# Second layer's input projection as a seven-product scheme, and its output projection as one sum

## The chip, the cores and the metric

One core of one Trainium2 chip. The metric is the device time of one execution in microseconds (us), median of the runs shown. TensorE (PE) multiplies, VectorE (DVE), ScalarE (ACT) and GpSimd (POOL) do everything else on chip, and SyncE's queue (SP) issues most transfers.

## The reference, cut to what matters

Layer 1 (counted from 0) is the retention layer, and the change is there: h is 1024 tokens x 1024 features, w_in 1024 x 6144, w_out 2048 x 1024, with 4 heads whose q and k are 256 and v and g 512 wide. Layer 0 (differential attention) is not touched, but its last steps build the input of layer 1.

```python
def retention(h, w_in, w_out):
    proj = jnp.einsum("bsd,de->bse", h, w_in)
    q, k, v, g = jnp.split(proj, [1024, 2048, 4096], axis=-1)
    ...
    inner_out = jnp.einsum("bnhij,bnjhe->bnihe", inner, v)
    _, cross = lax.scan(step, state0, ...)
    out = head_rms_norm(inner_out + cross)
    y = jax.nn.silu(g.astype(f32)) * out
    return jnp.einsum("bse,ed->bsd", y.astype(h.dtype), w_out)

for layer in range(DEPTH):
    h = rms_norm(x, pre_gain[layer]) * (1.0 + scale) + shift
    y = mixer(h)
    x = x + gate * rms_norm(y, post_gain[layer])
```

## The kernel before, in words

Every float32 product is made of three fp16 products: each operand is split into a high part (`hi`, written by ACT) and a low part (`lo`, what is left, written by DVE), and the pairs hi-hi, hi-lo and lo-hi are added up in PSUM. A product over 1024 rows of the contraction is therefore 8 blocks x 3 = 24 matmuls of 128x128 weights and 512 moving columns.

Layer 0 ends with its output projection: `out0(t)` for 8 tiles of 128 tokens, 48 matmuls each (`outproj`, L551), then `residual`, a store of the new rows to DRAM (`x1_d`, a DMA issued by POOL) and their norm. `out0_hT(g)` (g = 0, 1: tiles 0 to 3 and 4 to 7) transposes the rows on PE (L297), and `modulate` applies scale and shift (ACT) and splits (ACT, DVE) into the tiles `hT`. The order of these steps is a string of letters (`order`); inside it, and everywhere else, a list scheduler fixes one order of instructions per engine when the kernel is built. Each engine then runs its own list first in, first out, and waits at a row whose inputs or buffers aren't ready.

Layer 1 works head by head (`retain`), two heads a half:
- `qk_T`: queries and keys of the head, 8 products of 24 matmuls with the weights stationary (`proj_T`, L306), N = 512 tokens;
- for each of six spans of tokens (`SPANS`): `scores` (L744), `values` (the v projection of a tile, `proj_N`, L318, 24 matmuls), `state` (L764) and `outputs` (L785, L795);
- `gate`: the g projection of each of 8 tiles (L318 again), then SiLU, times the output, and the split.

Layer 1's input projection is thus 4 heads x (8 + 8 + 8) x 24 = 2304 matmuls of 512 columns. Line 318 has 2304 in all as well, by chance: 1536 of them are layer 1's, and 768 of L306's 1392.

After each half, `out1_yT` transposes y by DMA and `outproj` multiplies with that half's 1024 rows of `ret_w_out`; half 0 writes its sum to DRAM (`part_d`), half 1 loads it, adds it (L865) and finishes with `residual`. That is 2 x 8 x 48 = 768 matmuls of 512 columns.

Buffers matter below: PSUM has banks `mm` (3), `sc` (2), `tr` (1), `av` (2), one 128x512 float32 each. In SBUF a `tag` is a ring of `bufs` slots, and a tile waits until its slot's last reader is done: the attention tiles `v` and the residual rows `xres` share the tag `v` (2 slots).

Of the kernel before, what the change touches and what calls it, by code (L numbers as in the profile page):

```python
# [79 lines left out]
def trunk(ctx: ExitStack, tc: tile.TileContext, a: dict, out: bass.AP):  # L81
# [4 lines left out]
    raws = ctx.enter_context(tc.tile_pool(name="raws", bufs=2))  # L86
    ws = ctx.enter_context(tc.tile_pool(name="ws", bufs=2))
    hts = ctx.enter_context(tc.tile_pool(name="hts", bufs=1))
    ys = ctx.enter_context(tc.tile_pool(name="ys", bufs=1))
    rows = ctx.enter_context(tc.tile_pool(name="rows", bufs=2))  # L90
    dram = ctx.enter_context(tc.tile_pool(name="dram", bufs=1, space=DRAM))
# [25 lines left out]
    part_d = dram.tile([P, NT, D], F32, name="part_d")  # L117
# [101 lines left out]
    def ada_gate(l, j):  # L219
# [108 lines left out]
    l0 = ctx.enter_context(ExitStack())  # L328
    att = l0.enter_context(tc.tile_pool(name="att", bufs=2, reuse_waits="tile"))
# [568 lines left out]
```

## Time and profile before

| | |
|---|---|
| median of 3 runs | 1398.25 us (1396.84 to 1399.16) |
| the profiled execution | 1397.34 us, span 1395.6 us |
| PE busy | 1337.2 us (96%) |
| DVE, ACT, POOL busy | 797.1 us (57%), 593.3 us (43%), 140.5 us (10%) |
| mean granted clock of PE | 0.995 |

The span is from the first to the last instruction; the 1.7 us beside it lie around the program. The share of busy time says which engine has no room; what ended an engine's idle time is read from the waits, and what a step takes from the timeline of its stretch.

### The profile page before, as it was taken

The numbers are of one execution on the slowest core, as the hardware profiler recorded it, in microseconds if no ns is written. First come the engines' busy times: TensorE is split into PE (matmuls) and PEld (weight loads), VectorE is DVE, ScalarE is ACT, GpSimd is POOL, SyncE is SP. The second block draws the span as 40 slices with busy tenths as digits, with TensorE's granted clock in tenths as the row PEclk, the third lists the DMA queues.
The fourth block names the chain that finished last, engine by engine and source line by source line (L and its number), as shares of the span: only waits on it lengthen the run. The fifth ranks groups of instructions, "written<-read, shape, count | busy, mean of one in ns | idle before, by whom it ended". The sixth has DMA issues, their size and how long they took to land.

```text
span 1395.6 us, 18378 instructions
## 1 busy us (share of the span) xinstructions
PE 1337.2 (96%) x7049; PEld 652.5 (47%) x7049; DVE 797.1 (57%) x1636; ACT 593.3 (43%) x1160; POOL 140.5 (10%) x278
## 2 busy tenths in 40 slices
PE   3899999999999998999999999999999999999997
PEld 2445455445545444444444444444444444444443
DVE  4866996997887777563663255420126632554443
ACT  4854544653644655473452234321224422343211
POOL 2000110101101222210000000100000000000011
PEclk9999999999999999999999999999999999999999
DMA  9823554556442466642310230334333102304274
GB/s 301 246 66 70 131 119 113 146 128 135 102 129 52 120 153 131 169 146 89 98 54 15 76 99 0 94 94 120 99 99 99 47 18 76 98 1 121 61 196 136
DMA packets 230953, 148.23 MB, mean 106 GB/s; under 512 B 141721, under 2 KB 219729, under 8 KB 230865
## 3 DMA queue, kind: packets, MB, share of 16 engines
q1 hardware_dynamic: 226608, 131.84, 35.9%
q0 software_dynamic: 4256, 15.21, 3.3%
q8 instruction: 55, 0.90, 0.3%
q14 instruction: 34, 0.27, 0.1%
HBM read 99.85 MB, written 12.58 MB: 81 GB/s over the span
## 4 chain that ended last, share of the span: by engine, by line
PE 79%; DVE 9%; ACT 3%; DMA 3%; issue 3%; SPq 2%; POOL 1%; DVEq 0%; POOLq 0%; ACTq 0%
PE ps_mm L318 32%; PE ps_mm L306 16%; PE ps_mm L551 16%; DMA dT<-sb 2%; PE ps_mm L795 2%; PE ps_sc L764 2%; PE ps_av L785 2%; PE ps_av L523 2%; DVE sb L493 2%; PE ps_sc L489 2%; PE ps_sc L490 1%; DVE acc L160 1%; DVE sb L512 1%; PE ps_sc L744 1%; DVE sb L508 1%
## 5 line engine op out<-in xcount | busy, mean ns | idle before, releaser
L318 PE MATMUL ps_mm<-w,hT 128*128 128x512 f16 x2304 | 513.1, 379 | 0.0
L318 PEld LDWEIGHTS <-hT 128*128 128x128 f16 x2304 | 223.6, 98 | 257.6
L306 PE MATMUL ps_mm<-hT,w 128*128 128x512 f16 x1392 | 309.9, 379 | 0.8 <-ACT po L856 0.8
L551 PE MATMUL ps_mm<-w_o,yT 128*128 128x512 f16 x1152 | 256.2, 380 | 0.1
L306 PEld LDWEIGHTS <-w 128*128 128x128 f16 x1392 | 135.4, 98 | 157.4 <-ACT w L246 0.8
L551 PEld LDWEIGHTS <-yT 128*128 128x128 f16 x1152 | 112.6, 98 | 133.1 <-issue 2.8
L247 DVE SCALAR_TENSOR_TENSOR w<-raw,w 128x2048 f16<-128x2048 f32 (+1 forms) x52 | 92.1, 1794 | 92.1 <-ACT w L246 92.1
L500 ACT ACTIVATE sb<-sb,mx 128x128 f32<-128x128 f32 (+7 forms) x128 | 98.2, 768 | 64.0 <-DVE mx L493 63.5
L493 DVE CUSTOM_DVE_ANT_0 sb<-ps_sc,table 128x512 f32<-128x512 f32 (+3 forms) x128 | 73.3, 585 | 34.2 <-PE ps_sc L490 29.1
L246 ACT ACTIVATE w<-raw 128x2048 f16<-128x2048 f32 (+1 forms) x52 | 76.9, 1511 | 27.9 <-PE ps_mm L318 10.1
L489 PE MATMUL ps_sc<-ks,qs 128*128 128x512 f16 (+3 forms) x192 | 61.5, 327 | 5.8 <-DVE mx L493 5.6
L511 ACT ACTIVATE sb<-sb 128x896 f16<-128x896 f32 (+6 forms) x64 | 43.3, 679 | 55.8 <-DVE sb L508 55.6
L160 DVE SCALAR_TENSOR_TENSOR acc<-raw,cond,acc 128x256 f32<-128x256 f32 x140 | 65.7, 480 | 2.1
L523 PEld LDWEIGHTS <-dT 128*128 128x128 f16 x864 | 53.6, 99 | 27.3 <-DMA dT<-sb 18.7
L279 POOL TENSOR_SCALAR ss<-ss 128x1 f32<-128x1 f32 x48 | 15.6, 324 | 473.4 <-ACT junk L278 462.4
L490 PE MATMUL ps_sc<-kl,qs 128*128 128x512 f16 (+3 forms) x192 | 61.7, 327 | 0.0
L830 DVE TENSOR_TENSOR sg<-y,sg 128x512 f32<-128x512 f32 x32 | 22.1, 690 | 69.0 <-ACT sg L813 69.0
L725 ACT ACTIVATE vr<-ps_mm 128x512 f16<-128x512 f32 x32 | 19.1, 597 | 91.6 <-PE ps_mm L318 91.6
L726 DVE SCALAR_TENSOR_TENSOR vr<-ps_mm,vr 128x512 f16<-128x512 f32 x32 | 22.1, 689 | 62.9 <-ACT vr L725 62.9
L523 PE MATMUL ps_av<-v,dT 128*128 128x128 f16 x756 | 52.7, 219 | 5.4 <-DMA dT<-sb 5.4
L813 ACT ACTIVATE sg<-ps_mm 128x512 f32<-128x512 f32 x32 | 19.1, 597 | 90.1 <-PE ps_mm L318 90.1
L512 DVE SCALAR_TENSOR_TENSOR sb<-sb 128x896 f16<-128x896 f32 (+6 forms) x64 | 48.2, 754 | 10.9 <-ACT sb L511 10.8
(165 smaller groups left out, 1412.3 us busy)
## 6 DMA issues: line engine op xcount, KB each, us to landing
raw<-in_ret_w_in SPq DMA_DIRECT2D x24, 1024.0 KB, 5.4
raw<-in_ada_w SPq DMA_DIRECT2D x32, 512.0 KB, 6.8
raw<-in_da_w_in SPq DMA_DIRECT2D x16, 1024.0 KB, 5.5
raw<-in_ada_w SPq DMA_DIRECT2D x8, 1024.0 KB, 5.2
raw_o<-in_ret_w_out SPq DMA_DIRECT2D x8, 1024.0 KB, 5.0
x<-in_x SPq DMA_DIRECT2D x8, 512.0 KB, 7.5
raw_o<-in_da_w_out SPq DMA_DIRECT2D x4, 1024.0 KB, 5.2
xres<-in_x POOLq DMA_DIRECT2D x4, 1024.0 KB, 7.2
```

The costliest lines, as they stand in the source:

```text
L160: nc.vector.scalar_tensor_tensor(out=acc, in0=t[:, k, :], scalar=cond[:, k : k + 1], in1=acc, op0=ALU.mult, op1=ALU.add)
L246: nc.scalar.activation(out=hi, in_=t[:, k, :], func=AF.Copy, scale=SW)
L247: nc.vector.scalar_tensor_tensor(out=lo, in0=t[:, k, :], scalar=SW, in1=hi, op0=ALU.mult, op1=ALU.subtract)
L306: nc.tensor.matmul(ps, w[:, k, wi, lo : lo + P], hT[k][g][:, xi, :], start=(k == 0 and wi == 0 and xi == 0), stop=(k == NK - 1 and wi == 1),)
L318: nc.tensor.matmul(ps, hT[k][g][:, xi, j * P : (j + 1) * P], w[:, k, wi, :], start=(k == 0 and wi == 0 and xi == 0), stop=(k == NK - 1 and ...
L489: nc.tensor.matmul(ps[c][:, 0:n], qs[:, c, q], ks[:, c, k], start=True, stop=False)
L490: nc.tensor.matmul(ps[c][:, 0:n], qs[:, c, q], kl[c][:, k], start=False, stop=True)
L493: nc.vector.tensor_tensor_reduce(out=sb[:, c, k], in0=ps[c][:, 0:n], in1=table[:, S - L + lo : S - L + lo + n], scale=-es, scalar=(3.0e38 ...
L500: nc.scalar.activation(out=sb[:, c, 0:L], in_=sb[:, c, 0:L], func=AF.Exp, scale=-1.0, bias=mx[:, m0 + c : m0 + c + 1], accum_out=z[:, 4 * ...
L512: nc.vector.scalar_tensor_tensor(out=dh[:, 1, :], in0=sb[:, 0, 0:L], scalar=SD, in1=dh[:, 0, :], op0=ALU.mult, op1=ALU.subtract)
L523: nc.tensor.matmul(o[:, i * P : (i + 1) * P], dT[:, di * (t + 1) + kb, :], v[:, kb, vi, e], start=(kb == 0 and di == 0 and vi == 0), stop= ...
L551: nc.tensor.matmul(ps, yT(yi, k), wo[k // 4][:, k % 4, wi, n * 512 : (n + 1) * 512], start=(k == 0 and yi == 0 and wi == 0), stop=(k == NK ...
```

## The change

Layer 1's input projection is made of seven products of quarters where the plain scheme has eight. The 1024x1024 matrix h is cut in four quarters (512 features x 512 tokens: `A11`, `A12`, `A22` and the sums `N3`, `S1`, `M2`, `N4`; even tiles of 128 tokens are one half, odd tiles the other). A block of weights, 1024 rows x 512 columns (`Columns`: q and k of a head, or the two halves of its v, or of its g), is cut in four quarters of 512x256, with the sums `T1` to `T4`. `Quarters.product(n)` does one of the seven products; some share a PSUM bank (`chain` x, y, z) and go on adding where the last stopped, after ACT has copied the bank out (`kept`). Four results are put together by DVE additions.

- Per product and per half of its outputs: 4 blocks x 3 = 12 matmuls of 512 columns for q and k of heads 1 to 3; for head 0 (tokens in two groups) and for all v and g, 24 matmuls of 256 columns.
- The sums of weights are made by POOL, in float32, in the loaded blocks: four 128x1024 additions per `Columns` (`prepare`), 12 `Columns` in all. Blocks are split by ACT and DVE (128x1024 each, 7 per `Columns`); B22 is loaded twice. Weights are made ready three products ahead (`AHEAD`), loads start up to six ahead.
- The sums of h are made by DVE in `out0_hT`, in tiles `hq` that take the tag `v`, in place of `modulate`.
- v and g of a head are computed for all 8 tiles; the retention steps then run beside g's products, one span after each product.
- The output projection is one sum over 2048 rows at the end. `y` of heads 0 to 2 goes to DRAM (`y_d`) and comes back by DMA transposes from there; the last head's y is transposed from SBUF. `part_d`, its store, its loads and L865 are gone. `ret_w_out` comes in 16 loads of 512 KB, 8 MB in all, just ahead of it.

```diff
+        for k in range(4):
...
+            t = att.tile([P, 8, 256], F32, name="hq", tag="v", bufs=2)
...
+                nc.scalar.activation(out=t[:, 2 * i : 2 * i + 2], in_=ps, func=AF.Identity, scale=m[:, 1:2], bias=m[:, 0:1])
+            nc.vector.tensor_tensor(
+                out=t[:, 4:6], in0=t[:, 1:2].to_broadcast([P, 2, 256]), in1=t[:, 0:4:3], op=ALU.subtract
+            )
+            nc.vector.tensor_tensor(out=t[:, 6], in0=t[:, 0], in1=t[:, 5], op=ALU.subtract)
+            nc.vector.tensor_tensor(out=t[:, 7], in0=t[:, 2], in1=t[:, 6], op=ALU.subtract)
+            for src, dst, sign in (
+                (t[:, 0:4:3], lambda b: hA[k // 2][:, k % 2, :, b, n], -1.0),
+                (t[:, 2], lambda b: hB[0][:, k, b, n], 1.0),
+                (t[:, 4:8], lambda b: hS[k][:, :, b, n], 1.0),
+            ):
+                nc.scalar.activation(out=dst(0), in_=src, func=AF.Copy, scale=sign)
+                nc.vector.scalar_tensor_tensor(out=dst(1), in0=src, scalar=sign, in1=dst(0), op0=ALU.mult, op1=ALU.subtract)
...
+    PRODUCTS = (
+        ("x", "A11", "B11"), ("y", "A12", "B21"), ("x", "M2", "T2"), ("x", "N3", "T3"),
+        ("x", "A22", "T4"), ("z", "S1", "T1"), ("z", "N4", "B22"),
+    )
...
+            add = lambda o, x: nc.gpsimd.tensor_tensor(out=r[o], in0=r[o], in1=r[x], op=ALU.add)
+            name = PRODUCTS[n][2]
+            if name == "T2":
+                add("B11", "B12")
+                add("B12", "B22")
+                add("B22", "B11")
...
+            if n in (0, 2, 3):
+                self.kept[n] = self.hold(n)
+                nc.scalar.activation(out=self.kept[n][0], in_=self.kept[n][1](src), func=AF.Copy)
+            elif n == 4:
+                self.done("21", src, -1.0)
+            else:
+                x, op = {1: (0, ALU.subtract), 5: (3, ALU.add), 6: (2, ALU.add)}[n]
+                dst, shape = self.kept[x]
+                nc.vector.tensor_tensor(out=dst, in0=shape(src), in1=dst, op=op)
...
+        for hs in ((0, 1, 2), (3,)):
+            for n in range(2):
+                for k in [4 * h + i for h in hs for i in range(4)]:
...
-                    nc.vector.tensor_tensor(out=po[:, sl], in0=ps[n], in1=po[:, sl], op=ALU.add)
```

Three pieces of the engines' lists show what moves. The first is ACT's list where layer 1 begins, after the last norm of layer 0: before, `ht` and `hT` are the last two feature blocks of `modulate` for tiles 4 to 7, `w` a split of weights and `qT`, `kT` the first results of the projection.

```order
L269 ACTIVATE ht_6117<-ps_sc,mod_6_3311 128x512
L269 ACTIVATE ht_6126<-ps_sc,mod_7_3478 128x512
L270 ACTIVATE hT<-ht_6117 128x512
L270 ACTIVATE hT<-ht_6126 128x512
L246 ACTIVATE w<-raw 128x2x256 x2
L697 ACTIVATE qT<-ps_mm 128x2x256 x2
L246 ACTIVATE w<-raw 128x2x256 x2
```

Now, at the same place, `hq`, `hA`, `hB` and `hS` are the last of four steps of `out0_hT(1)`, and the row of `held` takes the first product (n = 0) of tokens 0 to 511 out of its two banks.

```order
L629 ACTIVATE hq<-ps_sc,mod_3_2211 128x512
L629 ACTIVATE hq<-ps_sc,mod_7_3472 128x512
L640 ACTIVATE hA<-hq 128x2x256
L640 ACTIVATE hS<-hq 128x4x256
L640 ACTIVATE hB<-hq 128x256
L640 ACTIVATE hS<-hq 128x4x256
L807 ACTIVATE held<-ps_mm 128x256 x2
L772 ACTIVATE w1s<-raw_6161 128x4x256
L833 ACTIVATE qT<-held 128x2x128 x2
```

The first result of the projection stands behind all of `out0_hT(1)` in both, but it is now a row that PE waits for: in PE's list, whose piece from the change follows, the last transposes of layer 0's rows (`x`) stand ahead of the third product (n = 2, weights `w_6178`, quarter `hS`), which goes on in the bank that `held` is copied from.

```order
L310 MATMUL ps_sc<-ident,x_5730 128x128
L310 MATMUL ps_sc<-ident,x_5973 128x128
L310 MATMUL ps_sc<-ident,x_5805 128x128
L310 MATMUL ps_sc<-ident,x_6041 128x128
L799 LDWEIGHTS w_6178
L799 MATMUL ps_mm<-hS,w_6178 128x256
```

Before, PE's list had projections of tokens 0 to 511 between groups of these transposes and nothing that waited for ACT in that way. The last piece is SP's list at the start of the output projection: `raw_o` are loads of `ret_w_out`, `yT` the transposes of y, here before.

```order
L254 DMA raw_o<-in_ret_w_out 128x2x1024 x4
L840 DMA_TRANSPOSE yT<-y_8774 128x16x128
L859 DMA po<-part_d 128x1024
L840 DMA_TRANSPOSE yT<-y_8775 128x16x128
```

And now; the first `yT` are tile 1's, the third row of `yT` on is tile 0's, which takes the slot of `qT`.

```order
L1092 DMA raw1o<-in_ret_w_out 128x2x512 x6
L1125 DMA xr_12188<-x_d 128x1024
L1092 DMA raw1o<-in_ret_w_out 128x2x512 x4
L1106 DMA_TRANSPOSE yT<-y_d 128x12x128 x2
L1108 DMA_TRANSPOSE yT<-y_10860 128x4x128 x2
L1092 DMA raw1o<-in_ret_w_out 128x2x512
L1106 DMA_TRANSPOSE yT<-y_d 128x12x128
L1092 DMA raw1o<-in_ret_w_out 128x2x512
L1106 DMA_TRANSPOSE yT<-y_d 128x12x128
L1092 DMA raw1o<-in_ret_w_out 128x2x512
L1108 DMA_TRANSPOSE yT<-y_10860 128x4x128
```

Loads of weights, each of which waits for one of four slots, now stand between the transposes of the first tile.

## Rows read from the trace of the kernel before

**Rows 1.** Page, part 1: busy time of PE, share of the span, instructions.
```profile
PE 1337.2 (96%) x7049; PEld 652.5 (47%) x7049; DVE 797.1 (57%) x1636; ACT 593.3 (43%) x1160; POOL 140.5 (10%) x278
```

**Rows 2.** Waits of PE: line, releaser, us in total, times, longest.
```profile
PE ps_mm L306 <- ACT po L856: 0.8, 1, 0.8
PE ps_sc L297 <- DVE x L594: 0.7, 1, 0.7
```

**Rows 3.** Timeline of PE, last head of layer 1: start, us, line, shape, count.
```profile
1154.01 41.60 PE L306 MATMUL ps_mm<-hT,w 128*128 128x512 f16 x192
1195.45 1.15 PE L744 MATMUL ps_sc<-qT,kT 128*128 128x256 f16 x12
1196.44 10.52 PE L318 MATMUL ps_mm<-w,hT 128*128 128x512 f16 x48
1206.80 0.50 PE L744 MATMUL ps_sc<-qT,kT 128*128 128x128 f16 x6
1207.13 5.34 PE L318 MATMUL ps_mm<-w,hT 128*128 128x512 f16 x24
...
1304.09 83.54 PE L551 MATMUL ps_mm<-w_o,yT 128*128 128x512 f16 x384
```

**Rows 4.** Stretches of the last head: us, then busy by engine (instructions), clock, DMA.
```profile
1154.00:1195.40 41.40, 41.40 (x193) 18.80 (x192) 10.54 (x11) 8.89 (x11) 0.00 (x0) 1.00 0.23 64
1195.40:1304.00 108.60, 108.60 (x537) 51.13 (x536) 56.80 (x93) 42.37 (x73) 7.51 (x16) 1.00 0.24 71
```

**Rows 5.** Groups by line and shape: busy us, mean ns of one | idle before.
```profile
L247 DVE SCALAR_TENSOR_TENSOR w<-raw,w 128x2048 f16<-128x2048 f32 x36 | 81.9, 2288 | 90.5 <-ACT w L246 90.4
L271 DVE TENSOR_TENSOR hT<-ht,hT 128x512 f16<-128x512 f32 x32 | 21.1, 687 | 10.6 <-ACT hT L270 10.6
L725 ACT ACTIVATE vr<-ps_mm 128x512 f16<-128x512 f32 x32 | 19.1, 597 | 91.6 <-PE ps_mm L318 91.6
L388 DVE SCALAR_TENSOR_TENSOR v<-ps_mm,v 128x256 f16<-128x256 f32 x32 | 13.4, 420 | 1.9 <-ACT tg L387 1.8
L385 ACT ACTIVATE v<-ps_mm 128x256 f16<-128x256 f32 x32 | 12.0, 374 | 24.9 <-PE ps_mm L318 24.8
L269 ACT ACTIVATE ht<-ps_sc,mod 128x512 f32<-128x512 f32 x16 | 11.5, 773 | 0.0
L580 DVE SCALAR_TENSOR_TENSOR yh<-y,yh 128x1024 f16<-128x1024 f32 x8 | 9.8, 1223 | 9.1 <-ACT yh L579 9.0
L579 ACT ACTIVATE yh<-y 128x1024 f16<-128x1024 f32 x8 | 8.4, 1051 | 13.6 <-DMA yT<-yh 8.4 <-PE ps_mm L551 4.1 <-PE ps_av L523 1.1
```

**Rows 6.** Timelines of PE, DVE and POOL where layer 0 ends.
```profile
614.36 0.82 PE L297 MATMUL ps_sc<-ident,x 128*128 128x128 f32 x6
621.74 0.44 PE L297 MATMUL ps_sc<-ident,x 128*128 128x128 f32 x2 [0.74 <-DVE x L594]
617.45 1.28 DVE L568 SCALAR_TENSOR_TENSOR xres<-x,rs,xres 128x1024 f32<-128x1024 f32 x1
619.03 0.53 POOL L592 DMA_DIRECT2D x_d<-xres  x1 [1.16 <-DVE xres L568]
```

**Rows 7.** DMA issues by line: count, KB each, median us to landing.
```profile
raw_o<-in_ret_w_out SPq DMA_DIRECT2D x8, 1024.0 KB, 5.0
x_d<-xres POOLq DMA_DIRECT2D x8, 512.0 KB, 3.8
yT<-y SPq DMA_TRANSPOSE x16, 4.6
```

**Rows 8.** A stretch after a long wait of PE, columns as in rows 4.
```profile
540.00:550.00 10.00, 10.00 (x64) 5.89 (x63) 7.09 (x18) 5.21 (x13) 1.68 (x5) 0.74 0.30 58
```

**Rows 9.** Timeline of DVE at the end of the program.
```profile
1387.67 0.69 DVE L865 TENSOR_TENSOR po<-ps_mm,po 128x512 f32<-128x512 f32 x1 [2.87 <-PE ps_mm L551]
1390.89 1.41 DVE L568 SCALAR_TENSOR_TENSOR po<-po,rs,xr 128x512 f32<-128x512 f32 x2 [0.99 <-POOL rs L132]
```

**Rows 10.** Groups by line and shape, POOL: the largest operation that it has.
```profile
L348 POOL MEMSET kl<- 64x1024 f16 x16 | 15.1, 945 | 76.4 <-PE ps_sc L490 47.4 <-DVE hT L271 28.6 <-POOLq L884 0.3
```

More of the change, by code (lines that the diff above doesn't have):

```diff
@@ L453, in trunk @@
     qk_piece(1, "k", 1)
-    lv = att.tile([P, 4, 64], F32, name="lv", tag="tg", bufs=2)
+    lv = early.tile([P, 4, 64], F32, name="lv", tag="tg", bufs=2)
     for i, n in enumerate(("da_lambda_q1", "da_lambda_k1", "da_lambda_q2", "da_lambda_k2")):
@@ new lines, in bank_for, with queries_keys, hold, done @@
+    def bank_for(u):
+        return lambda chain: mm() if chain == "x" or u == 0 else tr()
+    def queries_keys(h, qT, kT, cols, m, toks):
+        n = toks.stop - toks.start
+        blocks = slice(toks.start // P, toks.stop // P)
+        def hold(_):
+            t = held().rearrange("p b e -> p (b e)")[:, 0:n]
+            return t, lambda x: x
+        def done(q, src, sign):
+            dst = (qT, kT)[q[1] == "2"]
+            u = slice((q[0] == "2") * P, (q[0] == "2") * P + P)
+            hi, lo = (dst[:, blocks, m, b, u] for b in range(2))
+            src = src.rearrange("p (c u) -> p c u", u=P)
+            nc.scalar.activation(out=hi, in_=src, func=AF.Copy, scale=sign * SQK1 / SPROJ)
+            nc.vector.scalar_tensor_tensor(out=lo, in0=src, scalar=sign * SQK1 / SPROJ, in1=hi, op0=ALU.mult, op1=ALU.subtract)
+        return Quarters(cols, [(slice(0, n), slice(m * P, m * P + P), toks)], hold, done)
@@ new lines, in trunk, with spare_part @@
+    last_y = {}
+    spare = []
+    def spare_part():
+        if not spare:
+            t = ret.tile([P, 2, 4, 2, 256], F16, name="w1s", tag="vr", bufs=2)
+            spare.extend(t[:, i] for i in range(2))
+        return spare.pop()
+    place0 = {5: spare_part, 6: spare_part}
+    for h in range(RET_HEADS):
+        retain(h)
+    wanted = list(dict.fromkeys((cols, n) for cols, n, _ in steps1))
+    AHEAD, LOADS = 3, 6
+    ready = loaded = 0
+    for cols, n, step in steps1:
+        at = wanted.index((cols, n))
+        while ready < min(at + AHEAD + 1, len(wanted)):
+            while loaded < min(ready + LOADS - AHEAD, len(wanted)):
+                wanted[loaded][0].load(wanted[loaded][1])
+                loaded += 1
+            wanted[ready][0].prepare(wanted[ready][1])
+            ready += 1
+        step()
```

392 lines of the change are left out of this document (261 added, 131 removed).

## The prediction

> **What bounds the kernel now.** The first view is the page's busy time: PE works 96% of the span [rows 1]. The second is the list of PE's waits: in layer 1 and on the way into it there are two worth naming, 0.8 and 0.7 us [rows 2]. So in that stretch a matmul less is time less, and a wait that appears is time more. The third is PE's timeline in the last head [rows 3], where each start follows the last end. From 1154.01 to 1195.45 us 192 matmuls of 512 columns run: 0.2158 us each. From 1195.45 to 1196.44 run six of 256 and six of 128; six of 128 alone take 0.33 us (1206.80 to 1207.13), so the 256-column ones take 0.66 / 6 = 0.109 us each, hardly more than half. The fourth view is the stretches of that head: DVE is busy 67.3 of 150 us, ACT 51.3 and POOL 7.5 [rows 4]. These have room on average; whether they have it at the right moment decides this case.
>
> **The change part by part.** The sum is made against the profiled execution, 1397.34 us, 0.9 under the median of the runs.
>
> *Matmuls of the input projection.* Before: 2304 x 0.2158 = 497.2 us. Now 7/8 of the work: heads 1 to 3 have 3 x 7 x 2 x 12 = 504 matmuls of 512 columns for q and k (108.8 us); head 0's q and k (336) and all v and g (2688) are 3024 of 256 columns (329.6 us). Together 438.4, so **-58.8 us**. All of it lies on the path, because PE never waits there. Short runs of 256 columns are all that rows 3 show; at 0.110 for 0.109 the term is -55.8.
>
> *Output projection.* 768 matmuls before and after. The two waits of rows 2 go with the work around them (-1.5), and the addition that follows the last matmul, 0.69 us [rows 9], leaves the tail: **-2.2 us** together. The stores and loads of the half sums were beside other work, and so are those of y that take their place, but for the first tile (below).
>
> *Way into layer 1.* Before, PE multiplied tokens 0 to 511 while tokens 512 to 1023 were made ready, and lost 0.7 us. Now its list has only the first two products of tokens 0 to 511 (48 x 0.109 = 5.2 us) and the 32 transposes (0.82 / 6 = 0.14 each, 4.4 us [rows 6]) ahead of the third product. That one goes on in a bank which ACT copies out, and that copy stands on ACT behind the whole of `out0_hT(1)`. When can ACT begin there? The first `hq` takes the slot of the rows of tiles 6 and 7, which their store must have read. The last matmul of layer 0 ends at 614.4 (where the six transposes of rows 6 start); the store is issued at 619.03 and lands 3.8 us on [rows 7]: 8.4 us after that matmul. ACT then has, for each of four k, two reads of PSUM with scale and bias (0.77 each) and splits of 512, 256 and 1024 columns (0.60, 0.37, 1.05): 3.6 us. DVE has subtractions of 512, 256 and 256 (0.69, 0.42, 0.42) and splits (0.69, 0.42, 1.22): 3.9 us, all from rows 5. DVE sets the pace: 8.4 + 1.5 (ACT's first two reads) + 4 x 3.9 - 1.2 (the last split isn't waited for) + 0.4 for the copy = 24.7 us after layer 0's last matmul. PE has 9.6 us of work in it: **+15 us**. `out0_hT(0)` has one slot and some 6 us per step beside the last two output tiles: **+1**. After so thin a stretch PE's clock is low for some time; in the 10 us after a wait in layer 0 it was 0.74 on average [rows 8], so 2.6 us were lost: **+2.5**.
>
> *Head 0's q and k.* Products on one chain alternate between two banks, each 12 x 0.109 = 1.3 us. ACT's copy of 256 columns takes 0.37, but a split of weights (1.05 [rows 5]) may stand ahead of it: 0.3 us at some ten boundaries, **+3**. For v, g and the other heads the other bank's product lasts 2.6 us, which covers both.
>
> *Weights.* Per head 21 splits of 1024 columns, ACT 1.05 and DVE 1.22 each [rows 5], for 6 of twice that: DVE +12 us, ACT +10. With the copies and additions of the products DVE comes to some 90 of 135 us per head. Cover: weights are ready three products ahead, 3 x 5.2 us. POOL's twelve additions per head have no row like them. The nearest is a fill of 1024 half-precision elements, 0.945 us [rows 10]. Less than that is excluded, since an addition reads two operands more and writes twice the bytes; three streams of twice the bytes are 5.7 us. I take three streams at the row's time, 2.8. POOL then works 34 + 7.5 us per head, and three in a row plus a split are 10.7 us, inside the 15.6: **0**. For a sum of 2048 float32 elements the Trainium skill's page "GPSIMD Engine Reference", section 3.1, gives 4497 ns; half of it, an estimate, is 2.2 us, and the sum would stay as it is.
>
> *Change of head.* What g's last products release comes in a burst: DVE has four operations of 2048 columns, 2.29 each [rows 5], and ACT as many, before the new head's copies. PE has 65 matmuls (14 us) before it needs the copy after n = 2. The burst depends on the norm of the last tile, so ACT waits for DVE inside it. Bounds: nothing, if all fits into 14 us, and 6 us, if DVE's 9.2 come one after the other behind that norm. I take the middle, 3 us, three times: **+9**.
>
> *Start of the output projection.* The last tile's output needs the banks of the one before (a copy and an addition, 0.60 + 0.69 [rows 5]); the other heads fill this with the next product, the last can't. Then tile 0's y comes into the slot of `qT`, whose last reader is that output: two DMA transposes one after the other, 4.6 us to landing for the 16 blocks of before [rows 7], here 12 blocks each from DRAM: 4.6 + 1.7. No row shows one from DRAM. **+8**, and **+1.5** for the clock, which is less than rows 8 since the wait is shorter.
>
> **Sum:** -58.8 - 2.2 + 15 + 1 + 2.5 + 3 + 9 + 8 + 1.5 = -21.0, so 1376.3, and with the runs' 0.9 above the profile **1377 us**.
>
> **The rivals.**
> - *The queues hold (fewer waits).* `out0_hT(1)` starts before the store lands, or its steps overlap better, and changes of head cost nothing: waits of 15 us for the 40. Then 1398.25 - 61.0 + 15 = 1352 us. For it: DVE and ACT are under 70% busy on average. Against: the order of ACT's rows, which a faster DVE can't change.
> - *The weights of the output projection are late.* 8 MB in 16 loads through four slots, ten or so of them issued before the end of g. A load of 1024 KB takes 5.0 us [rows 7], so the last six of 512 KB take some 15, and they stand in one queue with the transposes of tile 0. Tile 0 needs the last within 18 us of its start. 10 us more: 1387. Against: the first loads are split early.
> - *Slower: POOL's additions come too late.* Each product of sums waits for three additions in a row and a split. Beyond (15.6 - 2.3) / 3 = 4.4 us an addition that is longer than the cover, and PE waits at each of 12 `Columns`. Of the 21 us gained above 1.75 each would be left to lose: 5.0 us an addition is where nothing is gained, and at the bound of 5.7 it is 3 x 1.3 x 12 = 47 us, 1377 + 47 = 1424. DVE's splits, 2 x 7 for each `Columns`, and POOL read the same memory at the same time; no row of this trace shows two such streams together. The Trainium skill's page "SBUF — State Buffer", section "Who interferes with whom", says that a DVE instruction with two SBUF inputs and a GpSimd instruction that reads SBUF shut each other out for a whole instruction. By that rule an addition of 2.8 behind a split of 1.22 is 4.0 us, and behind one of 2.29 it is 5.1, so this rival would decide; no run here shows it yet.
> - *It isn't what it says:* excluded by PE's list, which has the 504 and 3024 matmuls.
>
> **How the numbers follow.** The forecast has 0.56 (1364 to 1392 by its own bounds: the change of head 0 to 6, the way into layer 1 ± 5), the fewer waits 0.20, the late weights 0.14, the late additions 0.10. The range, 1351 to 1398, leaves out the late additions and half of the fewer waits. What a measurement of this kernel can tell from no change is about 0.2%, 2.8 us. Faster by more than that: all of the first two, most of the third, 0.87 in all; slower: the late additions above their turning point, 0.08; the same: the rest, 0.05.
>
> **What would show it.** Right: PE busy near 1276 us; 256-column matmuls 0.109 apart; one wait chain on PE of about 15 us in all for ACT or DVE where layer 1 begins, with ACT's `held` as releaser; one of 6 to 8 us for `yT` ahead of the output projection; small waits at three changes of head. Wrong: waits of PE for splits of weights behind POOL's sums, at every `Columns`; additions over 4.4 us; 256-column matmuls over 0.115 apart (then 18 us are lost); or no wait at all where layer 1 begins.

## The result, and the profile after

The changed kernel takes **1404.72 us** (median of 6, 1402.77 to 1408.88) where the kernel before takes 1397.55 on the same chip: ratio 1.0057, 95% interval 1.0038 to 1.0075. It is slower by 7 us; 21 us faster was forecast, and the range ended at 1398. The profiled execution took 1402.77 us with a span of 1400.8, against 1395.6 before.

The page's busy times come first; the row answers to [rows 1].

```profile
PE 1299.1 (93%) x8273; PEld 776.8 (55%) x8273; DVE 929.3 (66%) x1734; ACT 670.0 (48%) x1250; POOL 261.0 (19%) x318
```

PE has 1224 matmuls more, is busy 38 us less, and its share has fallen from 96 to 93%. In PE's timeline, in the v projection of head 0, 48 matmuls of 256 columns run from 711.76 to 717.00: 0.109 us each, as in [rows 3].

```profile
711.76 5.40 PE L799 MATMUL ps_mm<-w,hA 128*128 128x256 f16 x48
717.00 2.79 PE L799 MATMUL ps_mm<-w,hS 128*128 128x256 f16 x24
```

So the saving of 58 us is there, and more than all of it is lost again. Part of the loss is inside the busy time, which fell by 38 us and not by 58: the mean granted clock is 0.981 where it was 0.995, and 1.4% of 1299 us is 18 us (an estimate). Where the rest went, PE's waits begin to tell (us in total, times, longest). Where [rows 2] had 1.5 us in all, there are now these:

```profile
PE ps_sc L968 <- DVE a L952: 12.7, 9, 2.5
PE ps_mm L799 <- ACT held L807: 12.0, 4, 6.1
PE ps_sc L310 <- ACT hq L629: 6.6, 8, 2.6
PE ps_mm L1120 <- DMA yT<-y_d: 4.2, 2, 4.0
PE ps_av L989 <- ACT y L1003: 4.1, 3, 1.6
PE ps_mm L562 <- DVE x L575: 3.6, 1, 3.6
PE ps_mm L562 <- DMA yT<-yh: 1.2, 1, 1.2
```

None of them is a wait for a weight `w`. The rest is the clock, in the stretches that the waits thin out (us, then busy by engine, granted clock, DMA share, GB/s; [rows 4] had 1.00 throughout):

```profile
556.40:624.70 68.30, 60.27 (x304) 28.79 (x303) 45.18 (x57) 32.62 (x58) 25.97 (x36) 0.93 0.49 128
624.70:691.00 66.30, 48.86 (x371) 39.30 (x370) 46.25 (x67) 34.86 (x63) 14.79 (x13) 0.85 0.23 68
760.00:780.00 20.00, 17.85 (x123) 12.33 (x123) 17.57 (x22) 8.05 (x16) 12.57 (x9) 0.91 0.15 41
```

The third row lies around one of the waits for `a`; the 20 us from 900 and from 1040, each around such a wait too, have 0.91 as well.

By stage, in the two profiled executions, the account is this (stage marks from PE's timeline; "forecast" is the sum of the prediction's terms):

| stage | forecast | measured | of what |
|---|---|---|---|
| matmuls | -58.8 | -58.2 | 0.109 us for 256 columns, 0.216 for 512 |
| layer 0's tail (from the 21 matmuls of `ps_av` that begin at 548.9, now 549.1, to its last matmul: 65.5, now 75.8) | +1 | +10.3 | `x` 3.6, `yT` 1.2, `hq` 1.1, clock 0.93 |
| way into layer 1 and head 0's q and k (66.1 us with 41 of work) | +20.5 | +25 | first `held` 6.1 and the `hq` waits before it, a second `held` 5.4, clock 0.85 |
| heads (531.0 us, work 506.8) | +9 | +24.2 | waits 17.7, clock at 0.91 after the longest |
| start of the output projection | +9.5 | +6.3 | `yT` 4.2, clock |
| tail, and the waits of [rows 2] | -2.2 | -2.7 | |

They add up to 4.9, and the spans differ by 5.2. The heads' work is 2688 x 0.1092 + 504 x 0.2158 + 4 x 25.7 for the rest of a head (108.6 of [rows 4] less 384 x 0.2158) + 1.7 for the gate's products (L241).

**What happens in the heads.** Three of the waits for `a` are 2.4 to 2.5 us, one beside g's products in each of the first three heads. In DVE's and POOL's timelines of one (`y` is a tile of the output times its norm, `w` a split, `a` and `aT` the weighted products q·k; `a` is read from the bank that PE's next products need):

```profile
758.75 0.55 POOL L140 TENSOR_TENSOR rs<-ss,negh 128x1 f32<-128x1 f32 x1
759.27 11.10 POOL L759 TENSOR_TENSOR raw<-raw,raw 128x1024 f32<-128x1024 f32 x4
...
757.40 1.22 DVE L773 SCALAR_TENSOR_TENSOR w<-raw,w 128x1024 f16<-128x1024 f32 x1
759.33 2.56 DVE L1007 TENSOR_SCALAR y<-y,rs 128x512 f32<-128x512 f32 x1 [0.71 <-POOL rs L140]
761.82 0.28 DVE L952 TENSOR_TENSOR a<-ps_sc,dec 128x128 f32<-128x128 f32 x1
762.02 0.67 DVE L976 SCALAR_TENSOR_TENSOR st<-st,ps_sc 128x512 f32<-128x512 f32 x1
762.61 2.57 DVE L773 SCALAR_TENSOR_TENSOR w<-raw,w 128x1024 f16<-128x1024 f32 x1
765.11 2.43 DVE L954 TENSOR_TENSOR aT<-a,aT 128x128 f16<-128x128 f32 x1
```

```profile
758.82 0.81 PE L968 MATMUL ps_sc<-y,kN 128*128 128x512 f16 x3
762.15 1.05 PE L968 MATMUL ps_sc<-y,kN 128*128 128x512 f16 x3 [2.52 <-DVE a L952]
```

PE's products for `a` are done at 758.8, and PE has 0.8 us of other work until it needs their bank. DVE gets to `a` at 761.8, because `y` stands ahead of it in the list, waits 0.71 us for the norm, and then takes 2.56 us where the same shape takes 0.49 with no addition beside it. The split of 1024 columns takes 2.57 for 1.22, `aT` 2.43 for 0.28: about one addition of POOL's (11.10 / 4 = 2.8) each. `a` and `st`, with one operand in PSUM, keep their 0.28 and 0.67. So DVE's instructions with two operands in SBUF, and this one with a single one, wait for the end of a whole addition. The Trainium skill's page "SBUF — State Buffer", section "Who interferes with whom", says the same of both kinds, the second where the operation uses both of DVE's ports; this trace agrees.

By lines and shapes (busy us, mean ns) the additions are under the 2.8 us assumed, and under the 4.4 from which weights would come late:

```profile
L759 POOL TENSOR_TENSOR raw<-raw,raw 128x1024 f32<-128x1024 f32 x48 | 126.8, 2642 | 186.7 <-DVE w L773 183.5 <-DMA raw<-in_ret_w_in 0.5
L773 DVE SCALAR_TENSOR_TENSOR w<-raw,w 128x1024 f16<-128x1024 f32 x82 | 121.8, 1489 | 88.7 <-ACT w L772 88.6
```

**What happens where layer 0 ends.** In POOL's, DVE's, ACT's and PE's timelines:

```profile
563.31 12.26 POOL L759 TENSOR_TENSOR raw<-raw,raw 128x1024 f32<-128x1024 f32 x4 [2.26 <-DVE w L773]
573.41 5.52 DVE L773 SCALAR_TENSOR_TENSOR w<-raw,w 128x1024 f16<-128x1024 f32 x3
606.09 1.45 ACT L629 ACTIVATE hq<-ps_sc,mod 128x512 f32<-128x512 f32 x2 [0.26 <-DMA x_d<-xres]
632.58 2.30 ACT L629 ACTIVATE hq<-ps_sc,mod 128x512 f32<-128x512 f32 x3 [1.17 <-DMA x_d<-xres]
648.09 0.64 ACT L807 ACTIVATE held<-ps_mm 128x256 f32<-128x256 f32 x2
677.32 1.06 ACT L772 ACTIVATE w<-raw 128x1024 f16<-128x1024 f32 x1 [5.93 <-POOL raw L759]
678.28 0.64 ACT L807 ACTIVATE held<-ps_mm 128x256 f32<-128x256 f32 x2
```

```profile
579.58 8.04 PE L562 MATMUL ps_mm<-w_o,yT 128*128 128x512 f16 x24 [3.60 <-DVE x L575]
639.73 1.11 PE L310 MATMUL ps_sc<-ident,x 128*128 128x128 f32 x4 [2.64 <-ACT hq L629]
648.51 1.87 PE L799 MATMUL ps_mm<-hS,w 128*128 128x256 f16 x8 [6.05 <-ACT held L807]
678.70 2.72 PE L799 MATMUL ps_mm<-hS,w 128*128 128x256 f16 x12 [5.41 <-ACT held L807]
```

The addition to `x` that frees layer 0's banks stands behind three splits of the first weights (573.4 to 578.9): PE waits 3.6 us. Layer 0's last matmul ends at 624.9. `hq` of tiles 4 to 7 begins 7.7 us later (8.4 in the prediction), released by the store as foreseen, and the first `held` ends 23.8 us later (24.7). The second `held` was not foreseen: on ACT it stands behind a split that waits 5.93 us for POOL's additions. And 12 matmuls of 256 columns take 2.5 us (678.70 to 681.21) where 1.3 is usual.

### The profile page after: what moved, and what is told of

Read it like the earlier page. It is cut to its first block, busy times and chain, and to the rows that moved or that the text cites. A ratio compares the mean times of both kernels' runs of the same rounds, so it can differ in the third digit from the quotient of the medians.

```text
span 1400.8 us, 21197 instructions
## 1 busy us (share of the span) xinstructions
PE 1299.1 (93%) x8273; PEld 776.8 (55%) x8273; DVE 929.3 (66%) x1734; ACT 670.0 (48%) x1250; POOL 261.0 (19%) x318
## 5 line engine op out<-in xcount | busy, mean ns | idle before, releaser
L773 DVE SCALAR_TENSOR_TENSOR w<-raw,w 128x1024 f16<-128x1024 f32 x82 | 121.8, 1489 | 88.7 <-ACT w L772 88.6
L331 PE MATMUL ps_mm<-w,hT 128*128 128x512 f16 x768 | 175.7, 379 | 0.0
L1120 PE MATMUL ps_mm<-wo,yT 128*128 128x512 f16 x768 | 167.8, 382 | 4.2 <-DMA yT<-y_d 4.2
L799 PEld LDWEIGHTS <-hS 128*128 128x128 f16 x1536 | 150.1, 98 | 20.9
L759 POOL TENSOR_TENSOR raw<-raw,raw 128x1024 f32<-128x1024 f32 x48 | 126.8, 2642 | 186.7 <-DVE w L773 183.5
L319 PE MATMUL ps_mm<-hT,w 128*128 128x512 f16 x624 | 142.2, 379 | 0.0
L799 PE MATMUL ps_mm<-w,hS 128*128 128x256 f16 x1152 | 130.3, 273 | 0.0
L331 PEld LDWEIGHTS <-hT 128*128 128x128 f16 x768 | 74.2, 98 | 82.5
L575 DVE TENSOR_TENSOR po<-ps_mm,gp 128x512 f32<-128x512 f32 x16 | 11.1, 691 | 132.0 <-ACT junk L574 132.0
L562 PE MATMUL ps_mm<-w_o,yT 128*128 128x512 f16 x384 | 93.4, 394 | 4.8 <-DVE x L575 3.6
L799 PE MATMUL ps_mm<-w,hA 128*128 128x256 f16 x768 | 86.6, 273 | 0.0
L169 DVE SCALAR_TENSOR_TENSOR acc<-raw,cond,acc 128x256 f32<-128x256 f32 x140 | 65.7, 480 | 7.8 <-DMA raw<-in_ada_w 6.2
```

The source lines that it names most:

```text
L169: nc.vector.scalar_tensor_tensor(out=acc, in0=parts[k], scalar=cond[:, k : k + 1], in1=acc, op0=ALU.mult, op1=ALU.add)
L319: nc.tensor.matmul(ps, w[:, k, wi, lo : lo + P], hT[k][g][:, xi, :], start=(k == 0 and wi == 0 and xi == 0), stop=(k == NK - 1 and wi == 1),)
L331: nc.tensor.matmul(ps, hT[k][g][:, xi, j * P : (j + 1) * P], w[:, k, wi, :], start=(k == 0 and wi == 0 and xi == 0), stop=(k == NK - 1 and ...
L562: nc.tensor.matmul(ps, yT(yi, k), wo[k // 4][:, k % 4, wi, n * 512 : (n + 1) * 512], start=(k == 0 and yi == 0 and wi == 0), stop=(k == NK ...
L759: add = lambda o, x: nc.gpsimd.tensor_tensor(out=r[o], in0=r[o], in1=r[x], op=ALU.add)
L773: nc.vector.scalar_tensor_tensor(out=w[:, :, 1, :], in0=r[name], scalar=SW, in1=w[:, :, 0, :], op0=ALU.mult, op1=ALU.subtract)
```

## The experiments

Two theories were set against each other; where an expectation uses a letter, it says what it makes of it. **A**: the loss in the heads is the lock between POOL and DVE, each addition of weights makes DVE's rows longer. **C**: it is the order of rows; whatever stands ahead of a row that PE waits for and isn't ready delays it, and the engine of the additions is of no account. In the diffs `issue_after` (and `behind`, which calls it) sets a row behind a named one in an engine's list and adds no wait. All ratios are to the kernel before, with 95% intervals; "tail", "way in" and "heads" are the stages of the table above, in us of the profiled execution.

**No additions** (`no_sums`).
```diff
-            add = lambda o, x: nc.gpsimd.tensor_tensor(out=r[o], in0=r[o], in1=r[x], op=ALU.add)
+            add = lambda o, x: None
```


> Leaves out POOL's 48 additions of weight quarters (T1 to T4 are then plain quarters); everything else is as in the change. Theory A (DVE and POOL wait for each other by whole instructions, so that the additions hold up DVE's copies that PE waits for): the 3.6 us wait for x in layer 0's last output tiles, the second 5.4 us wait for held and the three 2.5 us waits at the changes of head go, with the low clock behind them: 1404.7 - 5 - 4 - 5.4 - 1.5 - 3 x 4 = 1377 us, +-6. Rival B (the waits come from how much DVE and ACT have to do there and in which order, and the additions lie beside it): 1400 us or more, the same waits.

1390.28 us, ratio 0.9938 (0.9915 to 0.9961): 14.4 us less than the change, and between what A (1377) and B (1400 or more) had said. In the profiled execution, which at 1384.82 was the fastest of four: heads 517.5 (13.5 less), way in 57.4 (8.7 less: the second `held` is gone), and the splits are back at 1220 ns (DVE, by lines and shapes):

```profile
L773 DVE SCALAR_TENSOR_TENSOR w<-raw,w 128x1024 f16<-128x1024 f32 x82 | 99.9, 1220 | 92.9 <-ACT w L772 92.6
```

The tail got no shorter, 77.7: a wait of 7.8 us for layer 0's `yT` stands there now. The additions cost, then, but not all that is lost, and 4.4 us of waits for `a` stay.

**The additions in quarters** (`sums_in_four`), so that none holds the memory for long.
```diff
+            add = lambda o, x: [nc.gpsimd.tensor_tensor(out=r[o][:, j], in0=r[o][:, j], in1=r[x][:, j], op=ALU.add) for j in range(4)]
```


> Each addition of 128x1024 on POOL is cut into four of 128x256; the order on every engine stays. Theory A: a DVE instruction can then be held up by 0.7 us at a time, not 2.6, so the waits of 2.5 us at the changes of head shrink below 1.5 and the 3.6 us in layer 0 below 2; the additions in a row still take some 8 to 11 us, so the 5.4 us for held stay: 1404.7 - 12 = 1393 us, +-6. Rival B: 1405 or more, since nothing but POOL's instruction count changes.

1421.54 us, 1.0161 (1.0144 to 1.0178): slower still, where A had 1393; B's 1405 or more had the side right, but not the reason. The lock got shorter as A has it (splits 1277 ns for 1489; beside a quarter `y` takes 0.94 us and `aT` 0.81, for 2.56 and 2.43), yet the waits for `a` rose to 21.6 us. The rows of POOL, DVE and PE, and POOL's group:

```profile
767.75 13.28 POOL L759 TENSOR_TENSOR raw<-raw,raw 128x256 f32<-128x256 f32 x16
781.97 0.49 DVE L1007 TENSOR_SCALAR y<-y,rs 128x512 f32<-128x512 f32 x1 [5.62 <-POOL rs L140]
782.71 0.98 PE L968 MATMUL ps_sc<-y,kN 128*128 128x512 f16 x3 [4.30 <-DVE a L952]
...
L759 POOL TENSOR_TENSOR raw<-raw,raw 128x256 f32<-128x256 f32 x192 | 159.5, 867 | 173.4 <-DVE w L773 173.2 <-DMA raw<-in_ret_w_in 0.2
```

Sixteen additions in a row last 13.3 us for 11.1, and the norm `rs`, a tiny row, stands behind them on POOL. `y` waits for it on DVE, and `a` behind `y`.

**The additions on DVE** (`sums_on_dve`), which takes the lock away.
```diff
+            add = lambda o, x: nc.vector.tensor_tensor(out=r[o], in0=r[o], in1=r[x], op=ALU.add)
```


> The 48 additions move from POOL to DVE, in the same places. Theory A: 1.2 us each in DVE's own list in place of 2.6 us on POOL plus the hold-ups; no DVE instruction is stretched any more: 1390 us, +-8. Rival B: DVE has 58 us more to do where it is already late: above 1405, up to 1425.

1392.31 us, 0.9962 (0.9947 to 0.9977), inside A's 1390 +- 8. But the gain isn't where A has it: the way in is 58.9 and the tail 72.7, while the heads are as long as ever, 531.6, and the waits for `a` are 13.9 us, now for another reason (DVE, then PE):

```profile
754.40 1.23 DVE L759 TENSOR_TENSOR raw<-raw,raw 128x1024 f32<-128x1024 f32 x1 [2.19 <-DMA raw<-in_ret_w_in]
755.54 0.28 DVE L952 TENSOR_TENSOR a<-ps_sc,dec 128x128 f32<-128x128 f32 x1
755.88 1.44 PE L968 MATMUL ps_sc<-y,kN 128*128 128x512 f16 x3 [4.90 <-DVE a L952]
```

An addition costs DVE 1.22 us, and one that waits for its load holds `a` up. The lock went and the loss in the heads stayed: against A alone. It fits C, but DVE also has 59 us more to do here, and this run doesn't tell the two apart.

**`held` in memory that layer 0 leaves early** (`held_elsewhere`).
```diff
-    ws1 = l1.enter_context(tc.tile_pool(name="ws1", bufs=5, reuse_waits="tile"))
+    heldp = l1.enter_context(tc.tile_pool(name="heldp", bufs=5, reuse_waits="tile")); ws1 = l1.enter_context(tc.tile_pool(name="ws1", bufs=5, reuse_waits="tile"))
-    held = lambda: ret.tile([P, 2, 256], F32, name="held", tag="held", bufs=5)
+    held = lambda: heldp.tile([P, 2, 256], F32, name="held", tag="held", bufs=5)
```


> The tiles held (first results of the projection that ACT copies out of PSUM) lie over memory that layer 0 leaves early, not over w_o, which its last output tile reads; ACT's list then has held of the first three products of tokens 0 to 511 between the steps of out0_hT(1), not behind them. Theory: PE has 26 us of products of tokens 0 to 511 to put beside out0_hT(1): the waits for held of 6.1 us and for hq of 5.5 us shrink to 3 us or less in all, and the clock stays up: 1404.7 - 9 - 6 = 1390 us, +-5. Rival: DVE, which makes the sums of h one after the other, sets the pace there and the products run dry all the same: 1400 or more.

1398.61 us, 1.0007 (0.9997 to 1.0018), between the 1390 of the theory and its rival's 1400. The first `held` is no longer behind `out0_hT(1)`, the way in is 60.4 (5.7 less); in its place there is a wait of 6.1 us for the split `w1s`, whose memory was of the same pool.

**The first y into `kT`'s slot** (`first_y_in_kT`).
```diff
-        yT = ret.tile([P, 2, 16, P], F16, name="yT", tag=("qT", "kT")[t % 2], bufs=1)
+        yT = ret.tile([P, 2, 16, P], F16, name="yT", tag=("kT", "qT")[t % 2], bufs=1)
```


> The changed kernel with one swap: the transposed y of tile 0 takes the slot of kT and that of tile 1 the slot of qT, the other way round than in the change; the last output of head 3 reads qT but not kT. Theory: the 4.2 us wait for yT ahead of the output projection, and the low clock of 0.91 behind it, come from the slot alone: 1404.7 - 4.2 - 1.8 = 1399 us, +-2. Rival: the loads of output weights that stand in one queue with the transposes are late anyway: 1404 or more, with the wait for wo or yT still there.

1400.52 us, 1.0019 (1.001 to 1.0029). The output projection begins at 1217.5, ahead of the last output of the retention (its end: 1222.5), and the wait for `yT` is gone: 4 us, as the step on its start had the cause.

**The additions on DVE behind `aT`** (`sums_behind_scores`).
```diff
+            add = lambda o, x: behind(lambda: nc.vector.tensor_tensor(out=r[o], in0=r[o], in1=r[x], op=ALU.add))
...
+                last["a"] = nc.vector.tensor_tensor(out=at[:, 1, 0:w], in0=t32[:, 0:w], in1=at[:, 0, 0:w], op=ALU.subtract)
```


> As sums_on_dve, with one edge more: an addition of weights comes behind the scores (a, aT) that stand ahead of it in the program, so the additions for the next head's q and k no longer lie between the retention steps. Theory C: at a change of head it doesn't matter which engine adds; PE waits because the copy a of the scores stands in DVE's list behind a row that an addition holds up. Then the waits for a shrink from 13.9 to 4 us or less, and 3 x 4 us go with the clock: 1392.3 - 12 = 1380 us, +-4. Rival D: DVE has too much to do there, and the additions cost the same wherever they stand: 1390 or more, waits for another tile in place of a.

1395.99 us, 0.9984 (0.9975 to 0.9994), no better than on DVE where they were. The waits for `a` are still 14.0. C's 1380 failed, and the number is rival D's (1390 or more). At the three longest waits other rows had come ahead of `a`: the sums `acc` of the gate (L169), which wait for loads. The place that C had named was wrong.

**The first additions behind tile 3's rows** (`first_sums_later`), on top.
```diff
+        done_x = add(slice(0, D))
+        if t == 3: last["a"] = done_x
```


> As sums_behind_scores, and the additions for the first head's q and k (made while layer 0 ends) come behind the fourth output tile's residual addition on DVE. Theory C: in layer 0 too PE waits because x stands behind splits that wait for additions: the 4.2 us for x and the low clock behind it go, 1380 - 6 = 1374 us, +-4. Rival: as in no_sums, the transposes of y then wait for the transfers of layer 1's weights, 1380 or more.

1397.62 us, 0.9997 (0.9986 to 1.0009), for 1374 expected. The wait for `x` is gone (0.3) and the tail is still 75.7: `hq` alone now makes PE wait 5.7 us at once. So `x` was not what set the end of the tail.

**The first weights' loads after layer 0's last transposes** (`loads_after_layer0`; else the change).
```diff
+                with tc.issue_after(lastyT[0].ins if hasattr(lastyT[0], "ins") else lastyT[0]): self.raw[b] = raw_block(self.src(int(b[1]) - 1, int(b[2]) - 1))
```


> The changed kernel, with one kind of edge more: the loads of the first weights of layer 1 come behind the last transpose of y of layer 0 in SP's queue, so that no split, addition or load of layer 1 lies beside the output tiles 3 to 5 of layer 0. Theory: the 10.3 us by which layer 0's end is late (75.8 us from the last attention products for tile 6 to its last matmul, against 65.5 before) come from that early work of layer 1; the stretch falls to 68 us or less, and what it gains is partly lost behind it, since weights and sums then meet out0_hT on DVE: 1404.7 - 8 + 4 = 1400 us, +-6. Rival: the stretch stays at 74 us or more, because out0_hT(0) waits for its slots (the stores of the rows), whatever layer 1 does.

1410.08 us, 1.0089 (1.0074 to 1.0104): tail 80.0, with 9.8 us of waits for `hq` in it, as the rival had it. Taking the loads, the splits and the additions out of the tail does not shorten it.

**Four moves together** (`all_moved`): first_sums_later, the pool for `held`, priority for its copy, and the swapped slots.
```diff
+                with tc.high_priority(offset=1000): nc.scalar.activation(out=self.kept[n][0], in_=self.kept[n][1](src), func=AF.Copy)
```


> first_sums_later, held_elsewhere and first_y_in_kT in one kernel, and the copies held ahead of other rows on ACT. If the three places are independent: 1374 - 6 (held_elsewhere measured that) - 6 = 1362 us, +-6; the copies ahead of the splits on ACT take the second wait for held of 5.4 us too, so rather 1358. If a new wait appears where out0_hT(1) ends (w1s): 1368.

1387.7 us, 0.9926 (0.9906 to 0.9946); way in 52.9, heads 532.0. That is some 20 us above the least hopeful of the three numbers expected: a wait of 7.0 us for `w1s` came, and the heads lost as much as before. The rows ahead of `a` are seen here (DVE, then PE):

```profile
747.84 1.00 DVE L169 SCALAR_TENSOR_TENSOR acc<-raw,cond,acc 128x256 f32<-128x256 f32 x2 [1.48 <-DMA raw<-in_ada_w]
748.76 0.28 DVE L960 TENSOR_TENSOR a<-ps_sc,dec 128x128 f32<-128x128 f32 x1
749.10 0.81 PE L976 MATMUL ps_sc<-y,kN 128*128 128x512 f16 x3 [2.58 <-DVE a L960]
```

**The gate's sums behind `aT` too** (`gate_behind_scores`), on top.
```diff
-                            ada_gate(1, h)
+                            behind(lambda: ada_gate(1, h))
```


> all_moved, and the sums of the gate's condition (acc, which read loads of ada_w) come behind the scores too. Theory C, as mended: it's the order of DVE's list that costs; PE waits for a because it stands behind whatever row isn't ready, an addition first, then y, now acc. Waits for a fall from 14.2 to 6 us or less, and with the clock 3 x 3.5 us go: 1387.7 - 10 = 1378 us, +-4. Rival D: another row takes the place, the waits for a stay above 11 us and the time above 1384.

1380.94 us, 0.9876 (0.9859 to 0.9892). The waits for `a` fall from 14.2 to 5.1 us and the heads to 526.6, though nothing of the work on DVE was taken away; rival D, which had 1384 or more, falls. The gate's own products, which had waited for nothing, now wait for the sums (PE's waits):

```profile
PE ps_tr L241 <- DVE acc L169: 5.5, 4, 1.6
```

So over half of what the waits for `a` lost has come back at another row.

**The first weights in memory that is free early** (`first_weights_early`), on top: `qT`, `kT`, `vr` and what shares their slots in a pool `reta`.
```diff
+    reta = l1.enter_context(tc.tile_pool(name="reta", bufs=1, reuse_waits="tile")); ret = l1.enter_context(tc.tile_pool(name="ret", bufs=1, reuse_waits="tile"))
...
+            t = reta.tile([P, 2, 4, 2, 256], F16, name="w1s", tag="vr", bufs=2)
...
+            with tc.high_priority(offset=1000 if n in self.place else 0):
```


> gate_behind_scores, and the slots of qT, kT and vr (the sixth and seventh weights of the first head lie there) in a pool of their own over w_o's memory, not in the pool whose end lies over hq; their splits ahead on ACT. Theory: the wait of 7.0 us for w1s where layer 1 begins is only that pool's and goes, for 1.5 us of clock more: 1378 - 7 = 1371 us, +-4. Rival: DVE then has them to split while it makes the sums of h, and the wait comes back for hq or hS: 1376 or more.

1374.47 us, 0.9829 (0.9812 to 0.9845). The wait for `w1s` is gone and the way in is 45.7.

**`out0_hT(0)` one tile later** (`h_one_tile_later`), on top: one letter of the order.
```diff
-        "o1 b5 a6 a7 b6 y4 o2 b7 f0 y5 o3 o4 y6 o5 h0 y7 o6 o7 h1"
+        "o1 b5 a6 a7 b6 y4 o2 b7 f0 y5 o3 o4 y6 o5 y7 o6 h0 o7 h1"
```


> first_weights_early, and the first half of the sums of h (out0_hT(0)) comes one output tile later in layer 0's order (o5 y7 o6 h0 o7 h1 for o5 h0 y7 o6 o7 h1). Theory: PE's wait of 5.5 us for hq in all_moved is for the slot that the store of tiles 4 and 5 must have read, and it goes with the later place: 1371 - 6 = 1365 us, +-5. Rival: the second half is then later by as much, and PE waits at the start of layer 1: 1371 or more.

**1371.73 us, 0.9816 (0.9796 to 0.9836)**: faster than both kernels, by 26 us than the one before. The tail is 65.7, as in the kernel before (65.5), for 76.1 in `first_weights_early`. What went is this (ACT, then PE, in `first_weights_early`; last PE here):

```profile
606.08 1.45 ACT L631 ACTIVATE hq<-ps_sc,mod 128x512 f32<-128x512 f32 x2 [2.42 <-DMA x_d<-xres]
606.91 1.12 PE L310 MATMUL ps_sc<-ident,x 128*128 128x128 f32 x4 [5.42 <-ACT hq L631]
...
604.80 0.66 PE L310 MATMUL ps_sc<-ident,x 128*128 128x128 f32 x4 [1.28 <-ACT hq L631]
```

So in this order the tail's loss was the place of `out0_hT(0)`: its `hq` needs a slot that the store of a pair of rows must free. The spans differ by 5.0 us only: half of the 10 us is given back on the way in, where more of `out0_hT` is now left to do, and the median is at the rival's 1371, not at 1365. The medians of the two runs differ by 2.7 us, which is within their spread; the step shows in the tail alone.

That is 33 us less than the change with all its work in place, and C seemed borne out. Two more runs asked what the additions still cost in this order.

**The additions back on POOL in the mended order** (`best_sums_on_pool`), behind the norms of each tile.
```diff
+            add = lambda o, x: behind(lambda: nc.gpsimd.tensor_tensor(out=r[o], in0=r[o], in1=r[x], op=ALU.add), "p")
...
                 r = row_rsqrt(src, RV, 1.0 / (SA * SV) ** 2, HEAD_EPS)
+                last["p"] = last["n"]
```


> The kernel of h_one_tile_later (1371.7 us) with its 48 additions back on POOL, everything else as there. Theory A (the lock between POOL and DVE costs wherever the additions lie: an addition is 2.64 us in which a DVE row beside it runs 2.4 to 2.6 us instead of 0.28 to 1.22): about 1.2 us more of DVE for each group of four additions on the rows that scores wait for, so 1376 us or more. Theory C (only the order of rows decides; with the rows that scores wait for ahead, whose engine adds is of no account): 1369 to 1374 us, within 3 us of 1371.7, the additions' 59 us of DVE being idle time won for nothing.

1406.92 us, 1.0068 (1.0052 to 1.0085): all is lost again. The engine matters, and C as put falls too; the place of the additions is another as well, since it is now one in POOL's list. The heads are 548.8 (22.4 more), the tail 8.9 and the way in 5.5 longer. At one change of head, POOL, DVE, ACT and PE:

```profile
777.55 0.56 POOL L140 TENSOR_TENSOR rs<-ss,negh 128x1 f32<-128x1 f32 x1
778.09 4.82 POOL L768 TENSOR_TENSOR raw<-raw,raw 128x1024 f32<-128x1024 f32 x2
778.15 2.56 DVE L1018 TENSOR_SCALAR y<-y,rs 128x512 f32<-128x512 f32 x1 [2.13 <-POOL rs L140]
782.94 1.06 ACT L782 ACTIVATE w<-raw 128x1024 f16<-128x1024 f32 x1 [4.84 <-POOL raw L768]
783.91 0.67 ACT L1013 ACTIVATE y<-ps_av,dec 128x512 f32<-128x512 f32 x1
784.63 0.59 PE L999 MATMUL ps_av<-vr,aT 128*128 128x512 f16 x1 [3.91 <-ACT y L1013]
```

The lock is back (2.56 for 0.49), the norm waits for an addition ahead of it on POOL, and on ACT the copy that frees PE's bank (`y`) stands behind a split that waits 4.84 us for the additions; waits for it rose from 4.2 to 14.0 us. Which share is the lock's and which is POOL's slower chain (2.36 and 4.82 us for three additions, 3 x 1.22 on DVE) this run does not separate.

**No additions in the mended order** (`best_no_sums`).


> The kernel of h_one_tile_later (1371.7 us) with the additions of weights left out: the sums of weights' quarters are replaced by plain quarters, so the output is not the reference's. It is a lower bound of what any place of the additions can give. Theory C (the additions are hidden once no row that TensorE needs stands behind them): 1368 to 1372 us. Theory A (they still take DVE's time beside the scores): 1360 to 1367 us; in no_sums, with the old order, leaving them out gave 14.4 us.

1378.51 us, 0.9867 (0.985 to 0.9884): 7 us *slower* with less work, which neither theory allowed. The heads did get shorter, 521.5 for 526.4: 5 us is what the additions still cost there. They are not shorter than the 517.5 of `no_sums`, though, so the mended order helps only with the additions on DVE. But the tail is 80.3, 14.6 longer, on one wait of 13.5 us for layer 0's `yT`. SP's timeline here:

```profile
568.91 3.56 SPq L736 DMA_DIRECT2D raw<-in_ret_w_in  x3
573.40 25.27 SPq L603 DMA_TRANSPOSE yT<-yh  x2
```

and with the additions, in `h_one_tile_later`:

```profile
573.51 11.68 SPq L603 DMA_TRANSPOSE yT<-yh  x2
```

Held behind tile 3's rows, the additions also held back the loads that need their slots. Without them three loads of 512 KB go out just ahead of two transposes, and the first of these lands only when PE's wait ends, at 594.6: 21 us after its issue, against a median of 4.3. In `no_sums` the same three loads and a wait of 7.8 us go together. The traces of the other runs bear this out: the transpose at this place lands 7.2 to 8.9 us after its issue in the ten (the kernel before among them) where no load of `w_in` stands just ahead of it, 10.4 to 13.1 in the four, the change among them, where two do, and 15.4 (`no_sums`) and 21.2 here. A load of `xres` that POOL issues with it takes 13.2 and 19.4 us in these two, and 7.6 to 9.1 in the ten, so the transposes alone are not what is slow there. In `loads_after_layer0`, which moves the loads behind them and nothing else, the transpose lands after 8.9 us, for 10.5 in the change.

## Why the prediction was wrong

*Right.* The matmuls (-58.2 for -58.8), the tail and the waits of [rows 2]. On the way in the first `held` with its place in ACT's list, when `hq` starts (7.7 us for 8.4) and when the copy comes (23.8 for 24.7); `first_y_in_kT` shows the cause of the wait for `yT`, which was 3 us smaller than forecast. The additions' duration: 2.64 us for 2.8.

*Wrong: "POOL then works 34 + 7.5 us per head, and three in a row plus a split are 10.7 us, inside the 15.6: **0**."* PE never waits for a weight, so the cover that was named held. What the step left out is what stands beside and behind an addition: DVE's rows are locked out for one, the norm queues behind four, and ACT's split waits for them with a copy behind it. Leaving the additions out gave 13.5 us in the heads and 8.7 on the way in, of which the tail and the stages ahead of it gave back 4.5 in the profiled execution; by the medians it was 14.4. The lock was written down as a rival, but priced by the wrong victim, the weights' cover, and so with a threshold of 4.4 us an addition that was never reached. That rival's 1424 had the sign of the result and not its mechanism.

*Wrong: "Change of head ... **+9**."* The heads' loss is 24.2, of which 13.5 go with the additions. The 10.7 left (517.5 less 506.8 of work) is near the 9 by luck, since at the two changes of head that show a wait the waits are 1.2 (`y`) and 0.3 us (`held`). The rest lies beside g's products, where the retention's small rows share DVE with the splits of the next `Columns` and the gate: PE has 0.8 us of work until it needs `a`, which stands behind rows that aren't ready. The step asked whether DVE has the time (it has), not what stands in its list.

*Wrong: "`out0_hT(0)` has one slot ...: **+1**."* It measured +10.3; moving that step by one tile gives 10.4 of the tail back in the mended order. The one slot was seen, and its price taken as if ACT's and DVE's time per step were all of it; the wait is for a store of rows. In the change itself the longest wait there is the 3.6 us for `x`, but with that one gone (`first_sums_later`) the one for `hq` grew to 5.7 and the tail stayed as long. The move by one tile was not tried in the change alone.

*Too small:* the way in by 4.5 us, for the second `held` (5.4) and a clock of 0.85 over 66 us, where +2.5 had been taken from a single window. The clock is also most of why PE's busy time is 1299 us and not the 1276 that was to show the forecast right.

The misses add up: 9.3 + 4.5 + 15.2 - 3.2, less 0.5 for the tail and 0.6 more for the matmuls: 25.9 us, which takes -21.0 to +4.9.

What stays open: how the loss on POOL, in the change and in the mended order, divides between the lock and the longer chain; and why three loads just ahead of a transpose make it and its neighbours so late, since no run sets those three alone.

## What to carry to other kernels

A cover in microseconds says only that an engine has the time. Ask also what stands behind each new row in its engine's list: the tiny row that PE needs next is late whenever the row ahead of it waits for a load, for another engine or for memory, and here mending that order and the slots that rows wait for, with the additions on DVE, was worth 33 us at the same work. Moving work to a half-idle engine isn't free where the two share memory, and cutting it into smaller pieces made it worse. When work is left out to measure its cost, look at what it had been holding back.

## What the runs showed of the hardware

- Beside a POOL addition of 128x1024 float32 (2.64 us), the DVE rows `aT`, `y` and `w`, with all their operands in SBUF, ended only after it: 0.28 became 2.43 us, 0.49 became 2.56, 1.22 became 2.57. Rows with an operand in PSUM kept their time. It holds the other way too: the additions with no DVE row beside them took 2.34 us, those that began while a split ran 3.2.
- A quarter of such an addition takes 0.867 us on POOL on average, not 0.66: sixteen in a row last 13.3 us, 3.3 for each four, where a whole one has 2.64. On DVE the whole one takes 1.22.
- After PE has waited, the granted clock stays under 2.4 GHz for a while: 0.91 on average in the 20 us around a wait of 2.5 us, 0.85 over the 66 us with waits of 6.1 and 5.4. Four float32 transposes that take 0.66 us took 1.11 after a wait of 2.64.
